# Two-layer transformer on one core: a fifth leaf of the MLP's Strassen products by inner products, and the first loads cut otherwise

## The chip, the core and the metric

The kernel runs as one program on one core of a Trainium2 chip. A core has a matrix engine (TensorE, PE in the profile, its weight loads PEld), VectorE (DVE), ScalarE (ACT), GpSimd (POOL) and SyncE (SP, which issues most DMA transfers). Each works through its own instruction list in order and waits on semaphores for the others. The metric is the device time of one execution in microseconds (us); given is the median of several executions.

## The reference

Two layers on 1024 tokens of width 1024 in float32: sliding-window attention with sinks, then a gated linear recurrence (HGRN2), each followed by an MLP with squared ReLU, and a last norm. What matters here is the MLP, which runs once in each layer:

```python
def rmsnorm(x, gain):
    y = xf * lax.rsqrt(jnp.mean(jnp.square(xf), axis=-1, keepdims=True) + NORM_EPS)
    return (y * gain.astype(jnp.float32)).astype(x.dtype)

def sqrelu_mlp(h, w_up, w_down):                     # 1024 -> 4096 -> 1024
    return jnp.square(jax.nn.relu(h @ w_up)) @ w_down

def reference(...):
    for layer in range(2):
        h = rmsnorm(x, mix_norm[layer])
        y = attention(h) if layer == 0 else hgrn2(h)
        x = x + y
        h = rmsnorm(x, mlp_norm[layer])
        x = x + sqrelu_mlp(h, mlp_w_up[layer], mlp_w_down[layer])
    return rmsnorm(x, final_norm)
```

## The kernel before

**Precision.** Every float32 operand is split into a high part in the fast float32r format and a low part, `lo = x - hi`, and a product takes three matmuls (`mm3`: hi*hi, hi*lo, lo*hi). Weights arrive by DMA in tiles `wr`; ScalarE casts the high part `wh`, VectorE subtracts to get the low part `wl` (`weight_split`, five buffers each). So each weight tile of 512 columns costs ScalarE one cast and VectorE one subtraction.

**Strassen in the MLP.** The up-projection goes over 16 pairs m of row blocks (m, m + 16) of 128 outputs each. One pair (`pair`) is a 2 x 2 Strassen-Winograd scheme with seven products (1 to 7), over output block, input half and token half. One product is four input tiles times three matmuls, so 12 matmuls with 512 token columns (`product`). The weight combinations s1 to s4 are made by VectorE in `m` buffers (six of them). The operands x[1] to x[7] on the token side are made once (`begin`, `finish`).

**Inner products.** From pair `INNER[layer]` on, some of the seven products are taken out of single pairs and done for two successive pairs at once by a second Strassen level. Such a *leaf* is called by the number of its product. For it the two weight blocks of both pairs (`up`, `low`) are combined by four half-width VectorE operations into four weight tiles ("12", "56", "73", "4"), and the four input tiles and two token halves into quarter operands (`inner_operands`). `inner_products` then does seven products of 2 x 3 matmuls of 256 columns, 42 instead of 2 x 12 of 512. After each of them VectorE adds the PSUM tile (128 x 256) to the sums of the pair. Before the change leaves 2, 3 and 4 are done so, from pair 2 on in layer 0 and from pair 4 on in layer 1. Leaves 2 and 4 keep their operands in SBUF; leaf 3 stores them to DRAM (`put_by`) and loads them into `t` buffers (18) for each use. In odd pairs leaf 2 and half of leaf 3 are done, in even ones leaf 4 and the rest of 3; the plain products 1, 5, 6, 7 stay in every pair.

**What sets the order.** The program is recorded as a list of operations with costs, and a planner (`Schedule`) places them engine by engine with list scheduling and several passes backward and forward. It knows the engines' costs, the hand-over times between them and the buffers, and takes a load as landed `LOAD` ns after its issue, a store as done `STORE` ns after it (3000 and 2000, behind an issue of 819 for 256 KB). Some operations may go to either of two engines: the squared ReLU of a sum (`square_relu`) is one operation on VectorE or two on ScalarE. The engines' lists are fixed when the program is built.

**Beginning and end.** The parameters (`par`: norm gains and lower bounds) come as 16 rows of 512 numbers by ScalarE's DMA queue, are turned into columns by four transposes on TensorE and copied to SBUF by ScalarE. Eleven dummy matmuls on zeros (`warm`) run ahead and between. Then the x tile of each input block is scaled by its gain on ScalarE (high part) and VectorE (low part), and the QKV products start; the first weight tile's high part is cast by VectorE. At the end (`final`) the last half block of 256 tokens is scaled in four tiles of 512 numbers per partition: one by GpSimd, which reads a copy of the scale factors that ScalarE makes from a second `spread` on TensorE, three by VectorE, one of them in two pieces; each piece has its own store.

In the profile all operations of the planner have line L433, so groups are told apart by tiles: `p` and `q` are the two sets of four PSUM banks, `wr`, `wh`, `wl`, `m`, `t`, `a` the buffers named above, `d` DRAM, `c` constants, `sm` small statistics.

Of the kernel before, what the change touches and what calls it, by code (L numbers as in the profile page):

```python
# [14 lines left out]
ALU = mybir.AluOpType  # L15
# [11 lines left out]
N_PAR = 8 * KT  # L27
# [109 lines left out]
LOAD, STORE = 3000.0, 2000.0  # L137
# [9 lines left out]
WARM = 11  # L147
ROWS = 16
EVACUATE = 100
HK = KT // 2  # L150
INNER = 2, 4
# [227 lines left out]
class Net:  # L379
# [129 lines left out]
    def weight_split(self, z, first=0, engines=("ACT",)):  # L509
        hi, lo = (self.tile(tag, BUFS[tag], (P, TH), F32R) for tag in ("wh", "wl"))  # L510
        c, n = slice(first, TH), TH - first
        self.copy(hi[:, c], z[:, c], n, engines, False)
        self.tt("any", lo[:, c], z[:, c], hi[:, c].bitcast(F32), ALU.subtract, n)
        return hi, lo
# [78 lines left out]
    def scaled(self, which, hf):  # L593

        h = []
        for kt in range(KT):
            x, gain = self.x[kt][hf], self.gain(which, kt)
            hi, lo = self.a(F32R), self.a(F32R)
            self.act(hi, x, AF.Copy, scale=gain)
# [9 lines left out]
    def square_relu(self, m, hf, c, psum):  # L609
# [6 lines left out]
        else:  # L616
# [7 lines left out]
            self.s.add({"ACT": (on_act, 2 * (94 + TH * 0.834) + 150), "DVE": (on_dve, 70 + TH * 1.04)}, [c], [c])  # L624
# [23 lines left out]
    def finish(self, which, upper_first=False, keep=False):  # L648

        x, t, q01, q11 = self.b, [], [], []  # L650
        self.u3 = []
# [6 lines left out]
        def lower():  # L658
            for j in range(HK):
# [3 lines left out]
                x[5].append(self.split(t[j]))  # L663

# [43 lines left out]
    def strassen_weights(self, first, second, done=(), inner=()):  # L708
# [15 lines left out]
        own = {2: a[0, 1], 3: s4}  # L724
# [12 lines left out]
        self.fourth = s4  # L737
# [4 lines left out]
    def inner_operands(self, own, kept, homes):  # L742
# [13 lines left out]
        new = lambda dt: self.t(dt, tag=next(homes))  # L756

        def split(name, z):
            y = self.split(z, new if homes else self.t)
            x[name] = [tuple(v[:, c] for v in y) for c in (L, R)] if homes else self.put_by(y)  # L760
# [28 lines left out]
    def inner_products(self, leaf, w, x, sums, steps):  # L789
# [6 lines left out]
        for step in steps:  # L796
            for name in step:
# [12 lines left out]
                self.tt("DVE", z, z, ps, ALU.add, 2 * P)  # L810
# [18 lines left out]
    def pair(self, m, x, leaves):  # L829
# [10 lines left out]
        if leaves and odd:  # L840
            inner.append((3, (self.fourth, 3), four if last else four[:2], (6, 9, 10, 11)))
            if last:
                inner.append((4, (up[m - 1 + half][:, TH:], up[m + half][:, TH:]), four, (9, 11, 13, 15)))
# [3 lines left out]
        w = self.strassen_weights(up[m], up[m + half], ((1, 2) if m < FIRSTS[self.layer] else ()) + ((2, 3, 4) if leaves else ()), inner)  # L847
# [37 lines left out]
        self.product(side, w[5], x[5], True)  # L885
        p5 = read(side)
# [3 lines left out]
        if leaves:  # L890
            self.tt("DVE", u2, u2, p5, ALU.add)
            self.sums[3].append((m, u2))
            if odd:
                z3 = self.rest = leaf(3, ((1, 2), (6, 5), (7, 3), (4,)))
# [19 lines left out]
        self.tt("any", p5, p5, u3, ALU.add)  # L914
        self.square_relu(m + half, 1, p5, False)
# [23 lines left out]
    def mlp(self, cut):  # L939

        x = self.mlp_second()
        for m in range(MT // 2):
            if m == INNER[self.layer]:
# [3 lines left out]
                                 4: self.inner_operands(self.b[4], self.u4, homes)}  # L947
                self.sums, self.rows = {2: [], 3: [], 4: []}, {}
# [46 lines left out]
    def down(self, cut):  # L995
# [99 lines left out]
        for c in (0, TH // 2):  # L1095
            tokens = slice(c, c + TH // 2)
# [78 lines left out]
    def first_loads(self):  # L1175
# [4 lines left out]
        rows = self.t()  # L1180
        self.op("ACT", self.nc.scalar.dma_start, [rows], [self.io["par"]], 100, rows[:ROWS], self.io["par"], tail=2900.0)
        ps = self.psum()
        n = N_PAR // ROWS
        for k in range(n):
            self.op("PE", self.nc.tensor.transpose, [ps], [rows, self.ident], 109, ps[:, k * ROWS : k * ROWS + ROWS],
                    rows[:ROWS, k * P : k * P + P], self.ident[:ROWS, :ROWS], form="whole")
        self.copy(self.par, ps[:, :N_PAR], N_PAR)
        for kt in range(KT):
            self.x[kt][0] = self.a()
            self.dma(self.x[kt][0], self.io["x"][0, kt], 4 * P * TH)  # L1190
# [6 lines left out]
    def qkv(self, hf, h, r, ahead=()):  # L1197

        blocks = range(hf * BPH, hf * BPH + BPH)
        for cg in range(3):  # L1200
            ps = {n: self.psum() for n in blocks}
            for kt in range(KT):
# [4 lines left out]
                w = self.weight_split(raw, engines=("ACT",) if kt or cg or hf else ("DVE",))  # L1207
# [679 lines left out]
```

## Time and profile before

| | us |
|---|---|
| median of 3 runs | 2060.28 (2060.0 to 2060.71) |
| the profiled execution, whole | 2058.19 |
| its span, first to last instruction | 2056.3 |
| TensorE clock granted (mean) | 0.999 |

| stage | about, us of the span |
|---|---|
| attention | 0 to 310 |
| MLP of layer 0, up-projection | 310 to 620 |
| its down-projection | 620 to 950 |
| HGRN | 950 to 1465 |
| MLP of layer 1, up-projection | 1465 to 1735 |
| its down-projection and the last norm | 1735 to 2056 |

The profile has several views. The page's head gives the busy time of each engine. *The chain of waits* goes back from the last instruction to what released it, and lists pieces as start, length, engine and tile, xcount. *Windows* give the busy time of each engine in a stretch. *Groups* collect equal instructions: busy time, mean ns of one, idle time of the engine before them and what ended it. *The timeline* lists instructions in order of time, equal ones merged. Matmuls overlap in the pipeline, so one's listed length is longer than its share of time; the pace is the length of a piece over its count.

### The profile page before, as it was taken

The page shows a single profiled execution, that of the slowest core. Times are in us where ns is not written, and L with a number is a line of the kernel's source. Part 1 is how long each engine was busy: PE and PEld are TensorE (multiplying, and loading weights), DVE is VectorE, ACT ScalarE, POOL GpSimd, SP SyncE. Part 2 cuts the span into 40 slices and gives each one's busy share as a digit, 9 for nine tenths or more (in the row PEclk, how much of TensorE's full clock was granted, in tenths as well). Part 3 has the DMA queues.
Part 4 walks back from the last instruction along what each step waited for, and adds up shares of the span by engine and source line. Part 5 has one row for each costly group of instructions (what it writes and reads, how often), then busy time and mean ns, then how long its engine had stood idle before and what let it go on. Part 6 is the DMA issues. An engine that isn't in the chain of part 4 may idle for free.

```text
span 2056.3 us, 35559 instructions
## 1 busy us (share of the span) xinstructions
PE 2046.4 (100%) x12150; PEld 1735.8 (84%) x12150; DVE 1845.8 (90%) x3699; ACT 1222.7 (59%) x2500; POOL 59.2 (3%) x121
## 2 busy tenths in 40 slices
PE   9999999999999999999999999999999999999998
PEld 8878888888898888888888888888888898888888
DVE  8899989999899979889988889998999899997985
ACT  7577977555565444666555555566765556444573
POOL 4030000000000000000000000000000000000000
PEclk9999999999999999999999999999999999999999
DMA  6212478877679978542333333688777677996812
GB/s 226 78 52 73 134 250 279 260 240 247 221 239 304 335 233 265 190 134 73 118 105 108 114 113 131 226 290 277 227 261 254 218 239 254 309 323 226 264 54 83
DMA packets 228486, 412.42 MB, mean 201 GB/s; under 512 B 25536, under 2 KB 30656, under 8 KB 228304
## 3 DMA queue, kind: packets, MB, share of 16 engines
q1 hardware_dynamic: 228272, 410.11, 60.0%
q8 instruction: 96, 1.57, 0.3%
q14 instruction: 86, 0.70, 0.1%
q10 hardware_dynamic: 32, 0.03, 0.0%
HBM read 319.34 MB, written 90.70 MB: 199 GB/s over the span
## 4 chain that ended last, share of the span: by engine, by line
PE 95%; DVE 2%; issue 1%; DMA 0%; ACT 0%; POOL 0%; POOLq 0%; DVEq 0%; ACTq 0%
PE p L433 49%; PE q L433 46%; DVE t L433 1%; DVE a L433 0%; DVE m L433 0%; DVE wl L433 0%; DMA d<-t 0%; DVE sm L433 0%; POOL a L433 0%; ACT m L433 0%; POOLq L1861 0%; ACT t L433 0%; DVEq L433 0%; POOLq L433 0%; ACTq L433 0%
## 5 line engine op out<-in xcount | busy, mean ns | idle before, releaser
L433 PE MATMUL p<-a,wh 128*128 128x512 f32 (+1 forms) x2680 | 751.9, 364 | 0.0
L433 PE MATMUL q<-a,wh 128*128 128x512 f32 x2180 | 673.8, 390 | 0.1
L433 PEld LDWEIGHTS p<-a,wh 128*128 128x128 f32 x2680 | 479.2, 189 | 78.5 <-DVE a L433 0.6
L433 PE MATMUL p<-a,wl 128*128 128x512 f32 (+1 forms) x1340 | 484.7, 362 | 0.0
L433 PEld LDWEIGHTS q<-a,wh 128*128 128x128 f32 x2180 | 402.7, 188 | 79.5 <-ACT t L433 0.5
L433 PE MATMUL q<-a,wl 128*128 128x512 f32 x1088 | 423.0, 389 | 0.0
L433 ACT CAST wh<-m 128x512 fp32r<-128x512 f32 (+1 forms) x336 | 205.3, 612 | 252.4 <-PE q L433 155.9
L433 ACT CAST wh<-wr 128x512 fp32r<-128x512 f32 (+1 forms) x323 | 194.6, 604 | 189.2 <-PE p L433 123.0
L433 PEld LDWEIGHTS p<-a,wl 128*128 128x128 f32 x1340 | 252.7, 189 | 37.2 <-DVE wl L433 0.4
L433 DVE TENSOR_TENSOR wl<-m,wh 128x512 fp32r<-128x512 f32 (+1 forms) x336 | 225.4, 676 | 55.4 <-ACT wh L433 51.1
L433 PEld LDWEIGHTS q<-a,wl 128*128 128x128 f32 x1088 | 204.3, 188 | 43.3 <-DVE wl L433 0.3
L433 DVE TENSOR_TENSOR wl<-wr,wh 128x512 fp32r<-128x512 f32 (+1 forms) x324 | 214.4, 665 | 21.3 <-ACT wh L433 19.0
L433 DVE TENSOR_TENSOR t<-t,t 128x512 f32<-128x512 f32 (+3 forms) x360 | 211.1, 607 | 15.1 <-ACT t L433 8.5
L433 DVE TENSOR_TENSOR a<-t,a 128x512 fp32r<-128x512 f32 (+1 forms) x317 | 209.1, 677 | 12.5 <-PE q L433 8.3
L433 ACT CAST a<-t 128x512 fp32r<-128x512 f32 (+1 forms) x237 | 141.6, 611 | 33.1 <-DVE t L433 10.6
L433 ACT ACTIVATE t<-t 128x512 f32<-128x512 f32 x196 | 123.6, 632 | 61.6 <-DVE t L433 58.1
L433 PE MATMUL p<-wh,a 128*128 128x512 f32 x384 | 124.8, 395 | 0.0
L433 DVE TENSOR_TENSOR m<-wr,wr 128x512 f32<-128x512 f32 (+1 forms) x186 | 120.3, 648 | 4.4 <-DMA wr<-in_down 3.1
L433 ACT COPY t<-q 128x512 f32<-128x512 f32 (+1 forms) x199 | 109.9, 558 | 23.2 <-PE q L433 11.5
L433 DVE TENSOR_TENSOR t<-t,p 128x256 f32<-128x256 f32 x273 | 111.3, 416 | 5.9 <-PE p L433 3.2
L433 ACT CAST a<-a 128x512 fp32r<-128x512 f32 x136 | 83.1, 620 | 49.5 <-DVE a L433 40.5
L433 DVE TENSOR_TENSOR a<-a,a 128x512 fp32r<-128x512 f32 (+2 forms) x151 | 101.0, 680 | 11.2 <-PE p L433 5.0
(135 smaller groups left out, 2428.2 us busy)
## 6 DMA issues: line engine op xcount, KB each, us to landing
t<-d SPq DMA_DIRECT2D x526, 256.0 KB, 4.3
d<-t SPq DMA_DIRECT2D x270, 256.0 KB, 3.0
wr<-in_down SPq DMA_DIRECT2D x224, 256.0 KB, 4.1
wr<-in_up SPq DMA_DIRECT2D x175, 256.0 KB, 3.9
a<-d SPq DMA_DIRECT2D x94, 256.0 KB, 4.6
wr<-in_win SPq DMA_DIRECT2D x68, 256.0 KB, 2.9
wr<-in_wqkv SPq DMA_DIRECT2D x48, 256.0 KB, 3.0
d<-a SPq DMA_DIRECT2D x48, 256.0 KB, 3.6
```

The lines of the kernel that those rows point to most:

```text
L433: fn(*[place(a) for a in args], **{k: place(v) for k, v in kw.items()})
```

## The change

1. **Fifth leaf.** Product 5 too is taken out of single pairs and done for two pairs by inner products, in the odd pair. Its operands are stored and loaded for each use, like leaf 3's (three of them; the others stay in SBUF), for which `finish` stores four more tiles (`u5`). The weight combination s1 of the even pair is held for the odd one (`self.fifth`). Four of its seven results are copied from PSUM by ScalarE (`fresh`), three are added by VectorE. The sums of both pairs are joined in the odd one (`upper_right`).
2. **Entry.** Layer 0 begins with leaves at pair 4 instead of 2; layer 1 as before at 4.
3. **Squares.** The squared ReLU of a sum goes to ScalarE alone.
4. **Planner.** `LOAD, STORE` from 3000, 2000 to 4200, 3200.
5. **Beginning.** The norm gains come as columns by one DMA (128 rows of 48 numbers), the lower bounds by a DMA of their own, later; transposes and copy go away. The first x tile is loaded and scaled in two halves, and the first weight tile's high part is cast half by VectorE, half by ScalarE. Nine dummies instead of eleven.
6. **End.** GpSimd's tile, the second `spread` and its copy go away for the last 256 tokens; VectorE does all four tiles, the first in two pieces.

```diff
-N_PAR = 8 * KT
+N_PAR = 6 * KT
-LOAD, STORE = 3000.0, 2000.0
+LOAD, STORE = 4200.0,3200.0
-WARM = 11
+WARM = 9
-INNER = 2, 4
+INNER = 4, 4
...
     def weight_split(self, z, first=0, engines=("ACT",), parts=False):
+        if parts:
+            for i, part in enumerate(PAIR):
+                self.copy(hi[:, part].only(i), z[:, part], TH // 2, engines[i : i + 1], False)
...
-            self.s.add({"ACT": (on_act, 2 * (94 + TH * 0.834) + 150), "DVE": (on_dve, 70 + TH * 1.04)}, [c], [c])
+            self.s.add({"ACT": (on_act, 2 * (94 + TH * 0.834) + 150)}, [c], [c])
...
     def inner_products(self, leaf, w, x, sums, steps, fresh=()):
-                self.tt("DVE", z, z, ps, ALU.add, 2 * P)
+                if name in fresh:
+                    self.copy(z, ps, 2 * P)
+                else:
+                    self.tt("DVE", z, z, ps, ALU.add, 2 * P)
...
         if leaves and odd:
-            inner.append((3, (self.fourth, 3), four if last else four[:2], (6, 9, 10, 11)))
+            inner.append((5, (self.fifth, 5), four, (5, 6, 7, 8)))
+            inner.append((3, (self.fourth, 3), four if last else four[:2], (9, 12, 13, 14)))
...
+        def upper_right(p5, n, u):
+            self.tt("any", p5, p5, u, ALU.add)
+            self.square_relu(n, 1, p5, False)
...
-        self.product(side, w[5], x[5], True)
-        p5 = read(side)
+        if not leaves:
+            self.product(side, w[5], x[5], True)
+            p5 = read(side)
+        elif odd:
+            early, p5 = (self.t() for _ in range(2))
+            run(self.inner_products(5, w, self.quarters[5], [early, p5], ((1, 2), (6, 5), (7, 3), (4,)), (1, 6, 5, 4)))
+            u = self.sums[3][-1][1]
+            self.tt("DVE", u, u, early, ALU.add)
+            upper_right(early, *self.sums[5][-1])
...
-        rows = self.t()
-        self.op("ACT", self.nc.scalar.dma_start, [rows], [self.io["par"]], 100, rows[:ROWS], self.io["par"], tail=2900.0)
-        ps = self.psum()
-        n = N_PAR // ROWS
-        for k in range(n):
-            self.op("PE", self.nc.tensor.transpose, [ps], [rows, self.ident], 109, ps[:, k * ROWS : k * ROWS + ROWS],
-                    rows[:ROWS, k * P : k * P + P], self.ident[:ROWS, :ROWS], form="whole")
-        self.copy(self.par, ps[:, :N_PAR], N_PAR)
+        self.op("ACT", self.nc.scalar.dma_start, [self.par], [self.io["par"]], 100, self.par, self.io["par"], tail=3000.0)
...
-        r, rs = self.spread(y, n), self.t()[:, :n]
-        self.copy(rs, self.spread(y, n) if ends else r, n)
+        r = rs = self.spread(y, n)
+        if not ends:
+            rs = self.t()[:, :n]
+            self.copy(rs, r, n)
...
-            e, share = ("DVE", r) if k else ("Pool", rs)
-            step = 1 if ends and k == per else per
+            e, share = ("DVE", r) if k or ends else ("Pool", rs)
+            step = 1 if ends and k == 0 else per
```

How the instructions move is shown at three places.

TensorE's list at the beginning of the program: dummies (from the zero tile `t`), the transposes of the parameter rows (to 128x16), then the first QKV products, four PSUM banks `p` each with matmuls on `wh` and `wl`. Before:

```order
L433 MATMUL p_178<-t_171 128x128 x6
L433 MATMUL p_208<-c_67,t_169 128x16 x4
L433 MATMUL p_178<-t_171 128x128 x5
L433 MATMUL p_243<-wh_214,a_225 128x512
L433 MATMUL p_243<-wl_222,a_225 128x512
L433 MATMUL p_243<-wh_214,a_236 128x512
L433 MATMUL p_253<-wh_214,a_225 128x512
L433 MATMUL p_253<-wl_222,a_225 128x512
```

After:

```order
L433 MATMUL p_177<-t_170 128x128 x9
L433 MATMUL p_225<-wh_215,a_220 128x512
L433 MATMUL p_225<-wl_218,a_220 128x512
L433 MATMUL p_234<-wh_215,a_220 128x512
L433 MATMUL p_234<-wl_218,a_220 128x512
L433 MATMUL p_239<-wh_215,a_220 128x512
L433 MATMUL p_239<-wl_218,a_220 128x512
L433 MATMUL p_225<-wh_215,a_230 128x512
L433 MATMUL p_234<-wh_215,a_230 128x512
L433 MATMUL p_239<-wh_215,a_230 128x512
```

The transposes and two dummies are gone. The first three banks take their matmuls with x's high part (`a_220`) first; those with its low part (`a_230`) follow.

TensorE's list in an odd pair of layer 1, a settled group: the first tile of leaf 2 (`wh`, `wl` of "12") times quarter operands `a`, into two banks. Before:

```order
L433 MATMUL p_20931<-a_17527,wh_20842 128x256
L433 MATMUL p_20931<-a_17548,wh_20842 128x256
L433 MATMUL p_20931<-a_17527,wl_20854 128x256
L433 MATMUL p_20931<-a_17541,wh_20842 128x256
L433 MATMUL p_20931<-a_17557,wh_20842 128x256
L433 MATMUL p_20931<-a_17541,wl_20854 128x256
L433 MATMUL p_20945<-a_17559,wh_20842 128x256
L433 MATMUL p_20945<-a_17566,wh_20842 128x256
L433 MATMUL p_20945<-a_17559,wl_20854 128x256
L433 MATMUL p_20945<-a_17572,wh_20842 128x256
L433 MATMUL p_20945<-a_17583,wh_20842 128x256
L433 MATMUL p_20945<-a_17572,wl_20854 128x256
```

After:

```order
L433 MATMUL p_20388<-a_17746,wh_20367 128x256
L433 MATMUL p_20388<-a_17776,wh_20367 128x256
L433 MATMUL p_20393<-a_17786,wh_20367 128x256
L433 MATMUL p_20393<-a_17802,wh_20367 128x256
L433 MATMUL p_20388<-a_17746,wl_20381 128x256
L433 MATMUL p_20388<-a_17761,wh_20367 128x256
L433 MATMUL p_20388<-a_17783,wh_20367 128x256
L433 MATMUL p_20388<-a_17761,wl_20381 128x256
L433 MATMUL p_20393<-a_17786,wl_20381 128x256
L433 MATMUL p_20393<-a_17794,wh_20367 128x256
L433 MATMUL p_20393<-a_17809,wh_20367 128x256
L433 MATMUL p_20393<-a_17794,wl_20381 128x256
```

Before, each bank's matmuls on the high and the low part of the weight alternate from the start. Now the first four rows are matmuls on the high part in both banks, and the first on the low part (`wl_20381`) comes behind them.

VectorE's list where layer 1's quarter operands are made (`t` with `t` at 256 columns, `a` the parts kept in SBUF) beside the weight tiles of the pairs that run (`wl`, `m`). Before:

```order
L433 TENSOR_TENSOR a_17548<-t_18109,a_17527 128x256
L433 TENSOR_TENSOR a_17557<-t_18109,a_17541 128x256
L433 TENSOR_TENSOR t_18109<-t_17914,t_18109 128x256
L433 TENSOR_TENSOR wl_18282<-wr_18063,wh_18273 128x512
L433 TENSOR_TENSOR t_18109<-t_17986,t_18109 128x256
L433 TENSOR_TENSOR m_18292<-wr_18075,wr_18222 128x512
L433 TENSOR_TENSOR a_18301<-t_18109,a_18294 128x512
L433 TENSOR_TENSOR t_18109<-t_17914,t_18109 128x256
L433 TENSOR_TENSOR t_18313<-t_18267 128x256
L433 TENSOR_TENSOR t_18313<-t_18138 128x256
L433 TENSOR_TENSOR m_18325<-wr_18222,wr_18279 128x512
L433 TENSOR_TENSOR wl_18332<-wr_18075,wh_18323 128x512
```

After:

```order
L433 TENSOR_TENSOR t_18484<-t_18365 128x256
L433 TENSOR_TENSOR wl_18489<-m_18459,wh_18479 128x512
L433 TENSOR_TENSOR a_17776<-t_18350,a_17746 128x256
L433 TENSOR_TENSOR a_17783<-t_18350,a_17761 128x256
L433 TENSOR_TENSOR t_18350<-t_18132,t_18350 128x256
L433 TENSOR_TENSOR t_18350<-t_18122,t_18350 128x256
L433 TENSOR_TENSOR t_18484<-t_18448 128x256
L433 SCALAR_TENSOR_TENSOR t_18450<-q_18211,t_18450 128x512
L433 TENSOR_TENSOR a_18530<-t_18350,a_18520 128x512
L433 TENSOR_TENSOR a_17563<-t_18484,a_17536 128x256
L433 TENSOR_TENSOR t_18350<-t_18132,t_18350 128x256
L433 TENSOR_TENSOR a_17572<-t_18484,a_17551 128x256
```

Before, operand work (`t_18109`, then `t_18313`) stands between weight work. Now two leaves' operands (`t_18350`, `t_18484`, the latter the new leaf's) stand in one row, with one weight operation among the twelve instead of four.

More of the change, by code (lines that the diff above doesn't have):

```diff
@@ L1094, in down @@
         yield 0, slice(0, TH)
-        for c in (0, TH // 2):
-            tokens = slice(c, c + TH // 2)
+        for tokens in PAIR:
             for m in range(HK):
```

69 lines of the change are left out of this document (44 added, 25 removed).

## Prediction

> **What bounds the kernel now.** I read the head of the page first, then the chain of waits, then the windows of the MLP's up-projection, then single rows at both ends.
>
> ```profile
> span 2056.3 us, 35559 instructions
> PE 2046.4 (100%) x12150; PEld 1735.8 (84%) x12150; DVE 1845.8 (90%) x3699; ACT 1222.7 (59%) x2500; POOL 59.2 (3%) x121
> PE 95%; DVE 2%; issue 1%; DMA 0%; ACT 0%; POOL 0%; POOLq 0%; DVEq 0%; ACTq 0%
> ```
>
> TensorE has work for the whole span, and 95% of the chain that ended last runs through it. A busy TensorE is not yet one at its pace, so the pace is read from the chain's pieces, which give a start, a length and a count:
>
> ```profile
> 786.98 43.52 PE p L433 x192
> 1570.81 2.87 PE p L433 x24
> 1573.68 2.75 PE q L433 x12
> 1576.42 2.15 PE p L433 x18
> ```
>
> The first piece is plain Strassen products of 512 tokens: 43.52/192 = 0.2267 us each. The others lie among the inner products of layer 1: 24 matmuls of 256 columns in 2.87 and 18 in 2.15, so 0.1195 each, and twelve of 512 columns in 2.75, 0.03 above 12 x 0.2267, once per change of width. These pieces follow each other without a hole, so TensorE sets the end and a removed matmul shortens the span. VectorE is the next engine. It has to deliver the low part of every weight tile:
>
> ```profile
> 1443.00:1480.00 37.00, 37.00 (x172) 30.55 (x171) 36.09 (x60) 27.73 (x51) 0.00 (x0) 1.00 0.69 224
> 1480.00:1517.00 37.00, 37.00 (x165) 30.63 (x164) 34.60 (x72) 26.70 (x52) 0.00 (x0) 1.00 0.81 274
> 1517.00:1554.00 37.00, 36.95 (x214) 32.39 (x213) 34.81 (x81) 21.56 (x39) 0.00 (x0) 1.00 0.78 251
> 1554.00:1591.00 37.00, 37.00 (x223) 33.08 (x222) 33.17 (x70) 20.10 (x36) 0.00 (x0) 1.00 0.70 233
> ```
>
> The columns after the length are the busy times of PE, PEld, DVE, ACT and POOL, then clock, DMA share and GB/s. In a settled stretch (the last row, about one group of two pairs) VectorE is busy 33.17 of 37; on entering layer 1's inner products (the first three) it has 0.9 to 2.4 us left in 37. So two things decide: how much matmul time goes, and whether VectorE still keeps ahead.
>
> **The change part by part. Matmuls.** A product of 512 tokens is 4 x 3 = 12 matmuls of 512 columns. By inner products two such products become 7 x 6 = 42 of 256. Layer 1 has six groups of two pairs and gains one leaf in each: 144 of 512 go, 252 of 256 come. Layer 0 had seven groups with three leaves (21) and now has six with four (24): 72 go, 126 come. Together 216 go, 378 come; the order has these counts. 378 x 0.1195 = 45.2 us come; 216 x 0.2267 = 49.0 go, or 49.5 at 2.75/12. That is -3.8 to -4.3. The changes of width from 512 to 256 fall from 133 to 126 in the order, worth 7 x 0.03 = 0.2, so I take **-4.0**.
>
> **The first 6 us.**
>
> ```profile
> 0.73 0.41 ACTq L433 DMA_DIRECT2D t<-in_par  x1
> 1.05 2.93 PE L433 MATMUL p<-t 128*128 128x128 f32 x12 [1.05 <-DVE t L433]
> 3.91 0.60 PE L433 MATMUL p<-c,t 16*128 16x16 f32 x4
> 4.00 0.61 DVE L433 CAST wh<-wr 128x512 fp32r<-128x512 f32 x1 [2.06 <-DMA wr<-in_wqkv]
> 4.44 2.01 PE L433 MATMUL p<-t 128*128 128x128 f32 x10
> 5.67 0.78 PE L433 MATMUL p<-t 128*128 128x128 f32 x5
> 4.79 0.72 ACT L433 ACTIVATE a<-a,c 128x512 fp32r<-128x512 f32 x1
> 6.20 0.48 PE L433 MATMUL p<-wh,a 128*128 128x512 f32 x1
> 6.79 0.72 ACT L433 ACTIVATE a<-a,c 128x512 fp32r<-128x512 f32 x1 [0.24 <-DMA a<-in_x]
> t<-in_par ACTq DMA_DIRECT2D x1, 32.0 KB, 2.9
> c<-in_pos SPq DMA_DIRECT2D x1, 4.0 KB, 4.7
> L433 ACT CAST wh<-wr 128x256 fp32r<-128x256 f32 x6 | 2.4, 407 | 1.5 <-PE p L433 1.5
> 2038.06 0.50 ACT L433 ACTIVATE a<-a,c 128x256 f32<-128x256 f32 x1
> ```
>
> Eleven dummies show as 22 passes, 12 before the four parameter transposes and 10 behind them; the first real matmul starts at 6.20, right behind the last dummy, though its operand was ready at 4.79 + 0.72 = 5.5. Twelve passes in 2.93 are 0.22 each; five in 0.78 from 5.67 on are almost twice as fast, so the array is slow until 5.67. Now there are nine dummies, 18 passes, and no transposes: 1.05 + 18 x 0.22 = 5.05. The operand: the first weight tile is there at 4.00, ScalarE splits its half in 0.41 and then makes the first half of x in 0.50, so 4.0 + 0.4 + 0.5 + about 0.1 = 5.0. The first real matmul starts at 5.05; until 5.67 it runs at half pace and loses 0.3. 6.20 - 5.05 - 0.3 = **-0.8**. The second x tile is issued one slot later (0.47 by the queue's rhythm), which can cost up to 0.4, and -1.1 is the gain with no slow stretch: bounds -1.1 and 0.
>
> The Trainium skill (TensorE: Matmul & The Clock Gate, Part 1) says that the warm-up is some 3.4 us of time and not a number of matmuls. The trace has 5.67 - 1.05 = 4.6 us, with transposes in between; by the page's figure the array would be fast before the last dummy and the term nearer -1.1, an estimate. The trace's own figure stays in the sum.
>
> **The end.**
>
> ```profile
> 2050.14 1.94 DVE L433 TENSOR_TENSOR a<-a,q 128x256 f32<-128x256 f32 x4 [0.87 <-PE q L433]
> 2051.03 1.27 POOL L433 TENSOR_TENSOR a<-a,t 128x512 f32<-128x512 f32 x1 [11.81 <-ACT t L433]
> 2038.59 14.67 SPq L433 DMA_DIRECT2D out<-a  x9
> ```
>
> GpSimd's tile, done at 2052.30, goes to VectorE, which is done with its own four at 2052.08 and takes 0.6 more: 2052.7. The last store was issued by 2053.26 and took 0.45 to issue, so from 2052.81; it now starts at about 2052.73: **-0.1**, bounds -0.2 and +0.3.
>
> **VectorE.**
>
> ```profile
> 1512.39 0.34 DVE a L433
> 1514.34 0.60 DVE wl L433
> L433 DVE SCALAR_TENSOR_TENSOR t<-t 128x512 f32<-128x512 f32 x13 | 8.9, 683 | 0.0
> L433 ACT CAST wh<-m 128x512 fp32r<-128x512 f32 x39 | 24.1, 619 | 33.9 <-PE q L433 21.3 <-issue 5.6 <-PE p L433 3.6
> 1528.49 0.68 DVE L433 TENSOR_TENSOR wl<-m,wh 128x512 fp32r<-128x512 f32 x1
> 1533.84 0.28 PE L433 MATMUL p<-t,wl 128*128 128x256 f32 x1
> ```
>
> Back to back a VectorE operation costs 0.60 at 512 columns and 0.34 at 256 (the chain's pieces). Per group there come three and a half low parts (2.1), four row sums (1.3) and three additions from PSUM (1.0); there go two low parts of the plain fifth products (1.2) and 13/3 squares, which are now ScalarE's alone (2.6). +0.7: 33.9 busy in a group that shrinks from 37.0 to 36.6 (72 x 0.2267 + 168 x 0.1195 + 6 x 0.03). ScalarE takes two activations for each square, four copies and the casts, some 7 us, to 27 of 36.6: hidden. ScalarE's own row says that its casts wait mostly for TensorE to give a buffer back (21.3 of 33.9), so VectorE in a settled group runs ahead as far as the five buffers let it. No wait there.
>
> The entry of layer 1's inner products is tighter. Priced row by row from the order, from the start of HGRN's output product to the first inner product, VectorE's work goes from 131.9 to 130.8 us and TensorE's from 152.7 to 147.5: the lead shrinks by 4.1, and at its lowest point in the pair behind it by 5.7. The smallest lead there is now 1533.84 - (1528.49 + 0.68) = 4.7 us, the last two rows. 4.7 - 5.7 leaves a wait of 1.0. VectorE's idle share there (2.2 to 2.4 in 37) can absorb some: I take **+0.7**, bounds 0 and 5.2 (the operands of the new leaf alone: ten of 0.34 and three of 0.60, if nothing absorbs them). Layer 0 enters two pairs later than before, behind pairs in which VectorE has half its time free: nothing there.
>
> **The transfers.** Three more stored operands of two tiles each are loaded per group: 1.6 MB on top of 233 GB/s x 37 us = 8.6 MB. The DMA share goes from 0.70 to about 0.84, which the second row above has (0.81) with TensorE unbroken. SP's later landings only reorder the issues: the plan gave a load 0.8 + 3.0 us.
>
> ```profile
> t<-d SPq DMA_DIRECT2D x526, 256.0 KB, 4.3
> ```
>
> It takes 4.3, so the plan was optimistic by 0.5 and TensorE did not wait for it; I cost it at nothing, with -2 (a wait or two less in attention and HGRN) and +2 as ends.
>
> **Sum.** 2056.3 - 4.0 - 0.8 - 0.1 + 0.7 = 2052.1 us of span. The profiled execution took 2058.19, 1.9 more than its span, and the median of the three runs is 2060.28; -4.2 on the median gives **2056.1**.
>
> **The rivals.** (B) *VectorE is late at layer 1's entry by 1.5 to 5 us.* For it: the three windows with 34.6 to 36.1 of 37, and the order, in which TensorE now takes the high-part matmuls of two banks before the first low part (second place shown with the change); against it: work before the entry can slip. With 3 us in place of 0.7: 2058.4. (C) *The parameters land late.* They come as 128 rows of 192 bytes. The only narrow load is c<-in_pos, 4.7 us against 2.9, though behind fourteen others. At 0.73 + 4.7 = 5.4 the half product ends at 5.9 and the first matmul starts at about 6.1: the first 6 us give 0.1, so 2056.8. The Trainium skill (DMA: Bandwidth & Descriptors, Specifications) puts the least transfer for full rate at 512 B; 24 KB are too little to tell by rate, and no run here shows it yet. (D) *The later landings remove waits elsewhere.* In HGRN the chain leaves TensorE for microseconds at a time:
>
> ```profile
> 1356.24 3.04 DVE t L433 x9
> 1362.25 0.65 PE L433 MATMUL q<-c,t 128*128 128x128 f32 x4 [0.73 <-DVE t L433]
> ```
>
> At the end of that stretch TensorE waits 0.73. A second wait of that length and some shorter ones gone, 1.8 us, would give 2054.3. Against it: this wait is on VectorE, and not on a landing. (E) *VectorE becomes the bound of every group.* If the 3.8 us that it idles in 37 cannot be filled, a group lasts 33.9 + 3.8 = 37.7 instead of 37.0: twelve times +0.7, and the thirteenth, all plain now (168 x 0.2267 = 38.1), +1.1, gives +9.5 where -4.0 stood: 2060.28 - 0.9 + 9.5 = 2068.9. It decides as soon as more than 36.6 - 33.9 = 2.7 of that idle time is not to be filled. Against it: the buffer waits of ScalarE above.
>
> **How the numbers follow.** About 0.2%, 4.1 us, is what a measurement here tells from no change; below 2056.2 counts as faster. Forecast 0.47 (2054.9 to 2057.0; 0.29 of it below the line, since the dearer 512 price and a lead that holds both lie on that side, 0.18 above), B 0.20, C 0.07, D 0.18, E 0.08. Faster 0.29 + 0.18 = 0.47; within 0.18 + 0.20 + 0.07 = 0.45; slower 0.08. The range: 2053.2 (D with a full startup gain) to 2060.6 (B at its far end); E lies outside.
>
> **What would show it.** 216 fewer matmuls of 512 and 378 more of 256 at 0.227 and 0.1195; the first p<-wh,a near 5.05; the last store issued near 2052.7 less what is gained. VectorE busy about 33.9 in a settled group with TensorE unbroken. Holes in front of matmuls on a low part between layer 1's first inner products and two pairs later are B; holes in every group are E, and would make the prediction wrong.

## The result and the profile after

| | before | after |
|---|---|---|
| median, us | 2060.20 (8 runs, 2059.55 to 2062.34) | 2054.83 (8 runs, 2054.41 to 2055.12) |
| ratio | | 0.9973, 95% interval 0.9964 to 0.9982 |
| the profiled execution, whole | 2058.19 | 2054.78 |
| its span | 2056.3 | 2053.0 |

The change is faster by 5.4 us in the median. 2056.1 was predicted, with a range of 2053.2 to 2060.6; 2054.83 lies in the range, just below the 2054.9 to 2057.0 that the prediction gives to the forecast itself. The profiled executions differ by 3.4 us only; where the other 2 us come from is the main question of the experiments.

The head of the page of after, and its chain of waits by engine:

```profile
span 2053.0 us, 36250 instructions
PE 2042.3 (99%) x12300; PEld 1740.3 (85%) x12300; DVE 1853.4 (90%) x3751; ACT 1289.1 (63%) x2647; POOL 56.1 (3%) x120
PE 93%; DVE 6%; issue 1%; ACT 0%; DVEq 0%; ACTq 0%
```

TensorE still sets the end. The pace comes from two pieces of the chain (start, length, engine and tile, count):

```profile
1704.72 5.75 PE p L433 x48
1906.28 43.52 PE p L433 x192
```

43.52/192 = 0.2267 for 512 columns, as before; 5.75/48 = 0.1198 for 256. In the traces there are 6772 product matmuls of 512 columns (6988 before) and 2464 of 256 (2086 before): the 216 and 378 of the prediction. They are worth 378 x 0.1198 - 216 x 0.2267 = -3.7 us.

The windows of a settled stretch of layer 1's inner products, four groups long: start and end, length, then the busy times of PE, PEld, DVE, ACT and POOL, clock, DMA share and GB/s. Before:

```profile
1554.00:1702.00 148.00, 148.00 (x889) 132.33 (x888) 133.10 (x277) 79.86 (x142) 0.00 (x0) 1.00 0.71 233
```

After:

```profile
1549.00:1695.40 146.40, 146.28 (x961) 134.18 (x961) 137.89 (x310) 103.37 (x194) 0.00 (x0) 1.00 0.86 283
```

Per group of 36.6 us VectorE is now busy 137.89/4 = 34.5 us and ScalarE 25.8; TensorE has 0.12 us of holes in four groups. The waits of TensorE in after (in total, times, longest):

```profile
PE q L433 <- DVE sm L433: 1.4, 1, 1.4
PE p L433 <- DVE t L433: 1.0, 1, 1.0
PE q L433 <- ACT m L433: 0.5, 1, 0.5
PE p L433 <- DVE a L433: 0.3, 1, 0.3
PE q L433 <- ACT t L433: 0.2, 1, 0.2
PE q L433 <- issue: 0.2, 1, 0.2
```

The first two are the last norm and the start. So the trace of after has few waits left that could be removed, none above 0.5 us outside its beginning and end. Its beginning:

```profile
1.05 4.21 PE L433 MATMUL p<-t 128*128 128x128 f32 x18 [1.05 <-DVE t L433]
3.82 0.40 ACT L433 CAST wh<-wr 128x256 fp32r<-128x256 f32 x1 [1.37 <-DMA wr<-in_wqkv]
4.29 0.91 ACT L433 ACTIVATE a<-a,c 128x256 fp32r<-128x256 f32 x2
4.91 0.77 PE L433 MATMUL p<-wh,a 128*128 128x512 f32 x1
6.36 0.63 PE L433 MATMUL p<-wl,a 128*128 128x512 f32 x1
6.79 0.53 PE L433 MATMUL p<-wh,a 128*128 128x512 f32 x1
7.16 0.39 PE L433 MATMUL p<-wl,a 128*128 128x512 f32 x1
```

The first product matmul starts at 4.91 instead of 6.20, as the prediction has it (5.05). But the array works at half pace until 7.16 (from 6.36 to 6.79 it takes 0.43 us from one matmul to the next, later 0.23), where the profile of before had it fast from 5.84 on, in the last dummies (the first instruction that takes the short time to the next one). The table follows a few places of the program through both traces:

| start of, us | before | after | difference |
|---|---|---|---|
| first product matmul | 6.20 | 4.91 | -1.3 |
| 13th | 9.06 | 8.77 | -0.3 |
| 193rd | 51.73 | 51.92 | +0.2 |
| last attention values | 264.90 | 264.58 | -0.3 |
| last inner product of layer 0 | 610.77 | 609.46 | -1.3 |
| last inner product of layer 1 | 1733.67 | 1730.07 | -3.6 |
| last matmul | 2050.27 | 2046.22 | -4.1 |
| end of the span | 2056.31 | 2052.97 | -3.3 |

Between these two executions the beginning brings nothing, the leaf brings what its matmuls are worth, and the end gives 0.7 back (some 0.45 of it only because the last four matmuls of the old end are gone, so that the last matmul is an earlier one).

### The profile page after: what moved, and what is told of

Same layout as the page of the kernel before. It is cut to its first block, busy times and chain, and to the rows that moved or that the text cites. A ratio compares the mean times of both kernels' runs of the same rounds, so it can differ in the third digit from the quotient of the medians.

```text
span 2053.0 us, 36250 instructions
## 1 busy us (share of the span) xinstructions
PE 2042.3 (99%) x12300; PEld 1740.3 (85%) x12300; DVE 1853.4 (90%) x3751; ACT 1289.1 (63%) x2647; POOL 56.1 (3%) x120
## 4 chain that ended last, share of the span: by engine, by line
PE 93%; DVE 6%; issue 1%; ACT 0%; DVEq 0%; ACTq 0%
PE p L433 50%; PE q L433 43%; DVE t L433 3%; DVE a L433 1%; DVE wl L433 1%; DVE m L433 1%; DVE sm L433 0%; ACT t L433 0%; ACT m L433 0%; ACT L433 0%; ACT wh L433 0%; ACT a L433 0%; DVEq L1892 0%; ACT sm L433 0%; DVEq L433 0%
## 5 line engine op out<-in xcount | busy, mean ns | idle before, releaser
L433 PE MATMUL p<-a,wh 128*128 128x512 f32 (+1 forms) x2832 | 781.1, 361 | 0.2
L433 PE MATMUL q<-a,wh 128*128 128x512 f32 x2020 | 625.9, 390 | 0.0
L433 PEld LDWEIGHTS p<-a,wh 128*128 128x128 f32 x2832 | 500.8, 189 | 79.0 <-ACT wh L433 1.0
L433 PEld LDWEIGHTS q<-a,wh 128*128 128x128 f32 x2020 | 375.0, 188 | 74.2 <-DVE a L433 0.2
L433 PE MATMUL q<-a,wl 128*128 128x512 f32 x1008 | 391.8, 389 | 0.0
L433 DVE TENSOR_TENSOR wl<-m,wh 128x512 fp32r<-128x512 f32 x354 | 234.6, 667 | 38.9 <-ACT wh L433 32.9
L433 DVE TENSOR_TENSOR wl<-wr,wh 128x512 fp32r<-128x512 f32 (+1 forms) x324 | 214.0, 665 | 18.6 <-ACT wh L433 17.2
L433 DVE TENSOR_TENSOR a<-t,a 128x512 fp32r<-128x512 f32 (+2 forms) x321 | 210.2, 674 | 18.0 <-ACT a L433 6.8
L433 ACT ACTIVATE t<-t 128x512 f32<-128x512 f32 x288 | 179.6, 631 | 69.1 <-DVE t L433 64.1
L433 ACT COPY t<-q 128x512 f32<-128x512 f32 (+2 forms) x174 | 95.2, 556 | 24.3 <-PE q L433 19.0
L433 PEld LDWEIGHTS q<-t,t 128*64 128x64 f32 (+1 forms) x2160 | 95.8, 144 | 13.5 <-issue 7.3
```

Source lines behind the costliest of these rows:

```text
L433: fn(*[place(a) for a in args], **{k: place(v) for k, v in kw.items()})
```

## Experiments: the parts alone

Four kernels beside one another: the new beginning alone, the new numbers in the planner alone, the fifth leaf alone (with its later entry in layer 0 and the squares on ScalarE), and the change once more. The numbers alone are one line:

```diff
-LOAD, STORE = 3000.0, 2000.0
+LOAD, STORE = 4200.0,3200.0
```

The leaf alone is the change with this line, the beginning and the end put back; the beginning alone is item 5 of the change put into the kernel before.

Expected of the leaf alone:

> The fifth leaf, layer 0's entry at pair 4 and the squares on ScalarE alone, on the kernel before; old beginning, old landings, old end. Sum (the forecast's own terms): -4.0 for matmuls and +0.5 to +0.7 for waits on VectorE, so -3.3 to -3.5 us against before. Landings or Beginning (the rest of the measured -5.4 comes from one of these): the same -3.4 here, since neither is in this kernel. If it shows -5 or more, the leaf alone explains the result and the term was too small.

Of the beginning alone:

> The beginning alone (parameters as columns, first x tile in halves, nine dummies) on the kernel before. Sum: -0.3 to -0.8 us; the first real matmul near 4.9 instead of 6.2. Beginning: -2 us, because the timed executions of before lose more at the start than its profiled one did. Landings: -0.3 as in the trace.

Of the planner's numbers alone:

> LOAD and STORE of 4200 and 3200 alone on the kernel before: no instruction added or removed, only another order. Sum: 0, within 0.5 us. Landings: -1.5 to -2 us, and runs that scatter less than those of before. Beginning: 0.

Of the change again:

> The changed kernel once more on the same chip, as the measure for the parts: all theories -4.5 to -5.5 us against before. Its profile is a second look at the first 8 us: if the moment at which the array becomes fast belongs to the kernel it is again near 7.2; if it is a matter of the execution it lies elsewhere.

| kernel | median, us (range, runs) | ratio to before, 95% |
|---|---|---|
| before | 2060.29 (2057.78 to 2064.37, 28) | |
| leaf alone | 2059.51 (2055.92 to 2062.69, 11) | 0.9984 to 1.0002 |
| beginning alone | 2059.44 (2057.78 to 2061.32, 11) | 0.9986 to 1.0004 |
| planner's numbers alone | 2059.59 (2058.30 to 2060.66, 11) | 0.9986 to 1.0004 |
| the change again | 2054.69 (2054.37 to 2055.37, 6) | 0.9959 to 0.9982 |

No part alone is told from before, and together they would make -2.3 where the whole makes -5.6. The leaf alone misses its expectation most: its fastest execution is 1.9 us under the fastest of before, its median 0.8 where 3.3 to 3.5 was expected (the interval just reaches 3.3). The beginning alone, -0.85, is just beyond the end of what "Sum" said (-0.8); the numbers alone, -0.7, lie between their two theories; the whole, -5.6, is just beyond the -5.5 expected. The ranges tell more than the medians: kernels with the old numbers scatter by 3.5 to 7 us, the numbers alone by 2.4, the change by 1.

## Experiments: the parts taken out

The second set takes one part out of the change at a time, so that with the first all eight combinations of leaf, beginning and numbers are there. The change with the old numbers is the line above read backward; the change with the old beginning is item 5 undone; beginning and numbers without the leaf are the two parts put into the kernel before. The fourth kernel is before itself, for the profile of another execution.

> The change with one line put back: LOAD, STORE = 3000, 2000 (fifth leaf, new beginning and new end stay). Theory Sum (each part is worth what it brought alone; the landings alone brought 0.7 us): 2055.4 us, scatter as narrow as the change's (1 us). Theory Leaf needs landings (the planner takes a load as landed after 0.8 + 3.0 us, the loads of stored operands take 4.3 to 4.5, and with the fifth leaf's loads on top VectorE and ScalarE start late by a different amount in each execution): 2057 to 2059 us, a scatter of 4 us or more, waits of VectorE and ScalarE for transfers of over 15 us in the trace where the change has some 14, and holes in TensorE's list of 0.3 to 1.6 us inside the MLPs; its fastest execution near the change's median.

> The change with the old beginning (parameters as 16 rows with four transposes, whole first x tile, eleven dummies); leaf, landings and new end stay. Theory Sum: the beginning alone brought 0.85 us, so 2055.5 us. Theory Beginning (the profiled execution of before had an early start by luck, its array at full pace at 5.7 us; two other executions of the same beginning reached it only at 8.7 and 9.0, and their 13th product matmul came at 10.6 us and not at 9.1): 13th product matmul at 10.6 us, median 2056.2 to 2056.8, scatter up to 1.5 us. Theory Landings alone decide: 2054.7 to 2055.0.

> The kernel before with the new beginning and with LOAD, STORE = 4200, 3200; no fifth leaf, old end. Theory Sum of the parts alone: 0.85 + 0.7 = 1.55 below before, 2058.7 us. Theory Leaf is worth its matmuls and no more once nothing waits: the change's median plus 3.8 to 4.0 for the 216 and 378 matmuls, minus up to 0.7 for the entry and the end: 2057.9 to 2058.6 us, scatter of 1 us. If the beginning and the landings by themselves bring the larger part of the 5.6 us: below 2057.5.

> The kernel before as it is, for the profile of another execution. If the profiled execution shown of before was a lucky one at its beginning: first product matmul at 6.6 to 6.9 us instead of 6.20, the array at full pace at 8.5 to 9.0 us instead of 5.67, the 193rd product matmul near 53.3 us instead of 51.73, span 2057 to 2060. If not: 6.2, 5.7, 51.7, and a span that differs only through waits further on.

All eight, with the time that VectorE and ScalarE wait for transfers in the profiled execution (summed over the rows of the view of waits), and the start of the 193rd product matmul:

| beginning | numbers | leaf | median, us (range, runs) | waits for transfers, us | 193rd matmul, us |
|---|---|---|---|---|---|
| old | old | no | 2060.29 (2057.78 to 2064.37, 28) | 28.1; again 39.0 | 51.73; again 53.90 |
| new | old | no | 2059.44 (2057.78 to 2061.32, 11) | 39.7 | 52.16 |
| old | new | no | 2059.59 (2058.30 to 2060.66, 11) | 10.8 | 53.59 |
| old | old | yes | 2059.51 (2055.92 to 2062.69, 11) | 47.2 | 53.27 |
| new | new | no | 2058.30 (2057.76 to 2059.07, 11) | 16.4 | 51.79 |
| new | old | yes | 2058.88 (2056.33 to 2062.37, 11) | 48.3 | 51.91 |
| old | new | yes | 2054.85 (2054.75 to 2056.70, 6) | 9.7 | 52.29 |
| new | new | yes | 2054.83 (2054.41 to 2055.12, 8) | 15.9 | 51.92 |

In the second set before had 2061.27 (22 runs); the ratios were 0.9979 to 0.9996 for the change with the old numbers, 0.9958 to 0.9982 with the old beginning, 0.9978 to 0.9996 without the leaf.

**The leaf needs the numbers.** With the new beginning and the old numbers the leaf brings 2059.44 - 2058.88 = 0.6 us, with the new numbers 2058.30 - 2054.83 = 3.5. In the other direction the numbers bring 1.1 us without the leaf and 4.1 with it. "Sum" falls, "Leaf needs landings" holds: median, scatter and waits came out as it said (only the fastest execution with the old numbers, 2056.33, stays 1.6 us above the change's median, and the largest hole of TensorE lies in HGRN and not in an MLP). And 2058.30 without the leaf is what the matmuls alone let expect.

The sizes are less sure than the direction, since these differences go across sets. Before itself had 2060.29 in the first and 2061.27 in the second. Taken each against the before of its own set (and the change from the first set, 2054.69), the leaf brings 1.5 us with the old numbers and 2.6 with the new, the numbers 2.1 without it and 3.2 with it. The traces leave out the beginning and the end if one goes from the 193rd product matmul to the first matmul of the last scale factors. Over that stretch the leaf takes 3.8 us away with the new numbers and the new beginning, 3.5 with the new numbers and the old beginning; with the old numbers it adds 1.1 and 1.0. Each is one execution against one, and the two executions of before differ by 2.1 us there.

The waits of the change with the old numbers show how; first some of the largest of VectorE and ScalarE for transfers (total, times, longest):

```profile
DVE m L433 <- DMA wr<-in_up: 3.5, 3, 2.0
DVE m L433 <- DMA a<-in_wg: 2.0, 1, 2.0
ACT a L433 <- DMA t<-d: 12.9, 15, 1.8
ACT wh L433 <- DMA wr<-in_up: 7.3, 7, 3.1
```

The place, in HGRN, from the timeline (start, length, engine and operation; in brackets the idle time before it and what ended it):

```profile
1328.90 0.69 DVE L433 TENSOR_TENSOR m<-wr,a 128x512 f32<-128x512 f32 x1 [1.96 <-DMA a<-in_wg]
1330.36 0.49 PE L433 MATMUL q<-t,m 128*128 128x128 f32 x2 [1.76 <-DVE m L433]
```

In after there is no row for wr<-in_up or a<-in_wg at either engine, and ScalarE's largest for stored tiles are these:

```profile
ACT wh L433 <- DMA t<-d: 2.1, 1, 2.1
ACT a L433 <- DMA t<-d: 2.0, 3, 1.1
ACT t L433 <- DMA a<-d: 1.3, 1, 1.3
```

A tile lands late, VectorE (or ScalarE) starts late, and TensorE behind it. TensorE's own rows name VectorE or ScalarE here and not the transfer, so the view of TensorE's waits alone doesn't show the cause. A second such stop of 0.88 us stands in this trace at 1559.60, in layer 1's inner products, behind a wr<-in_up that VectorE waited for until 1555.69. TensorE's waits add up to 8.0 us in this trace and to 3.6 in that of after, and the spans differ by 5.5. The new profile of before has the same chain of three engines:

```profile
395.23 0.42 DVE L433 TENSOR_TENSOR m<-m,wr 128x256 f32<-128x256 f32 x1 [2.83 <-DMA wr<-in_up]
397.62 1.30 ACT L433 ACTIVATE t<-t 128x512 f32<-128x512 f32 x2 [2.88 <-DVE t L433]
399.97 0.50 PE L433 MATMUL q<-a,wh 128*128 128x512 f32 x1 [1.59 <-ACT t L433]
```

The first profile of before has nothing at this place. The two executions have the same instructions, so they can be compared matmul by matmul: the second is 2.2 us behind at the 193rd product matmul, 1.75 more are lost at this place and 0.3 at a wait in HGRN, and the last matmul is 4.3 behind. So the beginning makes half of this difference and one late landing most of the rest. That the scatter of all the runs is made of the same two things is argued from this pair, not shown run by run.

The sum of the feeding engines' waits is not the time lost. The beginning alone has 39.7 us of them, and TensorE's own waits are 4.4 us there, against 4.0 and 6.1 in the two executions of before. With the leaf and the old numbers they are 6.6 and 8.0, in the four kernels with the new numbers 3.6 to 4.1.

**The old beginning has two outcomes.** Its kernels with the new numbers, which scatter little otherwise (the new beginning has 1.3 and 0.7 us there), fall into two groups: without the leaf four runs from 2058.30 to 2058.68 and seven from 2059.55 to 2060.66, with the leaf five runs from 2054.75 to 2055.19 and one at 2056.70. Five traces of this beginning have the array fast from 5.84 and 6.04 us on (193rd matmul at 51.73 and 52.29), or from 8.99, 8.99 and 10.56 (53.27 to 53.90). The new profile of before (span 2060.6, one run of 2062.46) has the late one that was expected, and later still, at 10.56:

```profile
4.04 0.58 PE L433 MATMUL p<-c,t 16*128 16x16 f32 x4
4.55 2.50 PE L433 MATMUL p<-t 128*128 128x128 f32 x10
6.70 0.77 PE L433 MATMUL p<-wh,a 128*128 128x512 f32 x1
8.98 0.63 PE L433 MATMUL p<-wh,a 128*128 128x512 f32 x1
```

In the two early ones the transposes follow the dummies at 3.91; in the three late ones at 4.04 to 4.18, and one of them names the reason, the profile of the new numbers alone:

```profile
4.18 0.58 PE L433 MATMUL p<-c,t 16*128 16x16 f32 x4 [0.20 <-DMA t<-in_par]
```

So parameters that are 0.13 to 0.27 us late go with an array that is slow for some 3 to 4.5 us more. Five traces show that the two go together, and not that one causes the other. The nine traces of the new beginning have the array fast between 4.38 and 7.17 (the change itself at 7.16 and, in its second profile, at 6.17, so the moment belongs to the execution and not to the kernel), and yet the 193rd matmul between 51.79 and 52.36. Where the array is early, here the kernel without the leaf, it stands still for the second x tile instead:

```profile
1.05 3.93 PE L433 MATMUL p<-t 128*128 128x128 f32 x18 [1.05 <-DVE t L433]
4.74 0.50 PE L433 MATMUL p<-wh,a 128*128 128x512 f32 x1
8.20 0.50 PE L433 MATMUL p<-wh,a 128*128 128x512 f32 x1 [0.46 <-ACT a L433]
```

The theory of the beginning was right about the two outcomes and wrong about how often: the change with the old beginning has a median of 2054.85 and not 2056.2 or more. By the median "Landings alone decide" came out; by their times five of the six runs had the early outcome and the one of 2056.70 the late one, but only one of the six was traced (an early one). So the new beginning is worth nothing against a good start and 1.4 to 2 us against a bad one.

## Experiments: which landing, later still, and the end

Three kernels change the planner's numbers in the change, the fourth puts the old end back (item 6 undone):

```diff
-LOAD, STORE = 4200.0,3200.0
+LOAD, STORE = 4200.0,2000.0
...
-LOAD, STORE = 4200.0,3200.0
+LOAD, STORE = 3000.0,3200.0
...
-LOAD, STORE = 4200.0,3200.0
+LOAD, STORE = 5000.0,4000.0
```

> The change with LOAD, STORE = 4200, 2000: only the planned end of a store is put back (after it a stored tile may be loaded again). Theory Loads decide (the waits that the old numbers left are of VectorE and ScalarE for tiles that come in, t<-d, wr<-in_up, a<-in_wg): 2054.7 to 2055.2 us, as the change. Theory Stores decide (stored operands are loaded again before their store is done): 2057 to 2059 us with 4 us of scatter, as with both numbers old (2058.88). Theory Both, half each: 2056 to 2057.

> The change with LOAD, STORE = 3000, 3200: only the planned landing of a load is put back. Theory Loads decide: 2057.5 to 2059 us, scatter of 4 us or more, over 30 us of waits of VectorE and ScalarE for transfers in the trace. Theory Stores decide: 2054.7 to 2055.2. Theory Both, half each: 2056 to 2057.

> The change with LOAD, STORE = 5000, 4000, later still. If the gain of the later landings is the removal of waits and these are gone (the change's trace has no wait of TensorE above 0.45 us outside its beginning and end): 2054.4 to 2055.2 us, no gain. If loads that land late still cost: below 2054.2. If buffers held longer bind (a load issued earlier holds its buffer longer): 2055.5 to 2058.

> The change with the old end (GpSimd takes one tile of four, four matmuls and a copy more). Theory of the prediction (the last store starts 0.1 us earlier with the new end): 2054.8 us, the old end 0.1 dearer. Theory Other way round (from the first matmul of the last scale factors to the end of the span it was 6.88 us in three traces with the old end and 7.16 in two of the new, with 2.04 less to the last addition or not; two other traces of the new end had 6.59 and 6.87): 2054.4 to 2054.6 us. Below 2054.3 it would beat the change by more than a measurement here tells.

| LOAD, STORE, end | median, us (range, runs) | ratio to before, 95% | waits for transfers, us |
|---|---|---|---|
| before in this set | 2060.46 (2057.91 to 2065.07, 22) | | |
| 4200, 2000, new | 2056.87 (2055.51 to 2057.36, 11) | 0.9974 to 0.9991 | 17.2 |
| 3000, 3200, new | 2057.69 (2054.68 to 2065.82, 11) | 0.9977 to 0.9999 | 37.5 |
| 5000, 4000, new | 2053.68 (2053.51 to 2054.55, 5) | 0.9952 to 0.9979 | 6.4 |
| 4200, 3200, old | 2054.86 (2054.35 to 2055.22, 6) | 0.9961 to 0.9984 | 14.8 |

**Both numbers count.** The old store costs 2.0 us, the old load 2.9, both together 4.1. For the store "Both" came out, for the load "Loads decide". The scatter comes with the load: 11 us against 2, or 4 without its two slowest runs (2063.98 and 2065.82), in which the granted clock was 0.996 and 0.997 instead of 0.999; what lowered it there was not recorded. With the old store the largest row of ScalarE's waits for transfers is for stores:

```profile
ACT t L433 <- DMA d<-t: 6.8, 8, 2.1
```

With the old load it is for loads of stored tiles:

```profile
ACT a L433 <- DMA t<-d: 12.6, 11, 3.6
```

These numbers move the whole order and not only the transfers, so a part of each 2 to 3 us may lie in other moves; that was not separated.

**Later still is faster.** 5000, 4000 gives 2053.68, 1.0 to 1.2 us below the change; only the slowest of its five runs is within the range of the change's fourteen, though the intervals against before overlap. The expectation by which no wait was left to remove missed by 0.7, and the one below 2054.2 came out. Its profiled execution is that slowest run, with one wait that the change hasn't, in front of HGRN:

```profile
PE p L433 <- ACT t L433: 1.0, 1, 1.0
```

Part of the gain can still be read from this trace: its 193rd matmul comes 0.4 us later than in after, its first inner product of layer 0 0.5 us earlier (400.37 against 400.88). Of after's small holes in attention (0.13 to 0.47 us, 0.9 in all, between 130 and 240 us) one of 0.21 is left. None of them can be followed back to a transfer in the trace of after, so this part seems to come from another order. Whether the other four runs lack the wait of 1.0 us no trace shows; without it this one would be at 2053.5, as they are. It is the fastest kernel of the study.

**The end is worth nothing.** 2054.86 against 2054.83 and 2054.69. The last matmuls, additions and stores of after:

```profile
2045.81 0.68 PE L433 MATMUL q<-c,sm 128*128 128x128 f32 x4 [1.36 <-DVE sm L433]
2046.53 2.54 DVE L433 TENSOR_TENSOR a<-a,q 128x256 f32<-128x256 f32 x5 [0.87 <-PE q L433]
2047.01 2.46 SPq L433 DMA_DIRECT2D out<-a  x5
```

And the matmuls of before:

```profile
2049.42 1.13 PE L433 MATMUL q<-c,sm 128*128 128x128 f32 x8 [1.36 <-DVE sm L433]
```

The last store is issued by 2049.47, 3.66 us behind the first of these matmuls; before it was 2053.26 - 2049.42 = 3.84. The 0.1 us of the prediction is there and a little more (0.18), and the landing and the closing instructions behind it take 0.45 longer in this pair of executions: 3.50 us from the last issue to the end of the span (2052.97 - 2049.47) instead of 3.05. Why, the profile doesn't show.

## Why the prediction was right, point by point

- **Matmuls, -4.0.** The counts are exact, the durations 0.2267 and 0.1198 in place of 0.1195: -3.7 and the changes of width.
- **VectorE, +0.7.** At layer 1's entry TensorE's excess over its pace (from the starts of its matmuls) is 0.18 us at 1526 and 0.29 at 1602, 0.5 in all. In the settled group VectorE is busy 34.5 of 36.6 (33.9 predicted), ScalarE 25.8 (27), and TensorE doesn't wait. Rival E is out, rival B too. Both terms together, -3.3, stand against 2054.83 - 2058.30 = -3.5 measured with the other parts in place (-2.6 if each is taken against the before of its set).
- **The first 6 us, -0.8.** The first product matmul came at 4.74 to 5.03 in all nine traces of the new beginning, so the timing of operands and dummies was right (2.93/12 is 0.24 and not 0.22, but the passes start 0.213 apart behind a first one of 0.375, which gives the same 5.05). The step "it runs at half pace until 5.67" took the moment at which the array becomes fast from one execution as if it belonged to the kernel. It moves between 4.38 and 10.56. The mean of the 193rd matmul is 52.96 us in five traces of the old beginning and 52.04 in nine of the new, -0.9; alone it brought 0.85 in the median (an interval that takes in zero), without the leaf and with the new numbers 1.3, in the whole 0. The size fits on the average, not in any one pair of executions, and that it does is luck. Rival C is out: the parameters landed in 3.3 us, from 0.73 on, and nothing waited for them.
- **The end, -0.1.** Not to be told from nothing.
- **Transfers and later landings, 0 (-2 to +2).** This is the step that failed. "the plan was optimistic by 0.5 and TensorE did not wait for it; I cost it at nothing": VectorE and ScalarE waited for transfers, 28 us in all in the trace of before, and stand in front of TensorE. That none of these waits can be followed on to a stop of TensorE in that trace was the luck of that execution; in the other one 1.6 us can. The numbers bring 0.7 us alone, 1.1 with the new beginning and 4.1 with the leaf (2.1 and 3.2 against the before of their sets), beyond the bound of -2. They also decide whether the -4.0 of the first term arrives: with the old numbers most of it doesn't (0.6, or 1.5). The term was priced as a part beside the others, and it is what the leaf stands on. In a settled group the DMA share went to 0.86 (0.84 predicted), from 0.71.
- **The base.** The sum was made against a span of 2056.3 and carried to a median 2.1 us above that execution, as if that distance stayed. It was, as far as the two executions of before show it, late landings and slow starts: the kernel with the new beginning and numbers alone has a median of 2058.30, the time of that execution (2058.19). The change takes them away, and all eight runs of after have spans of 2052.6 to 2053.3. In spans the sum was 0.9 too good (2052.1 against 2053.0), since this execution of before had the good beginning; in the medians it was 1.3 too poor. So the result lies within the range through a right leaf and, by luck, two errors that partly cancel: the beginning, which gave nothing in the profiled pair, and the base. Rival D, with its 2054.3, was nearest in size, and right in that later landings remove waits. Its example was not such a wait: in the trace of before VectorE works without a stop ahead of the 0.73 us at 1362.25, so the objection to it was right there. That wait is gone with the numbers alone all the same, by another order; the late landings that cost time were elsewhere. The range's lower end, 2053.2, takes the beginning off twice (2054.3 already holds 0.8 of the 1.1; it should be 2054.0), and the result is above both.

The 5.4 us of the medians can be put together in one order from the tables: beginning and numbers without the leaf 2060.29 - 2058.30 = 2.0, the leaf behind them 3.5, the end 0. Against the before of the second set the first part is 3.0 (2061.27 - 2058.30), which leaves 2.4 for the leaf, so this split is good to about 1 us.

## What to carry to other kernels

When an engine that feeds the bounding one waits for transfers, look at its waits too, even if the bounding engine shows none: not all of that time is lost, but it shows where an added load can turn a late landing into a stop, and a change that adds loads and one that issues loads earlier are to be priced together. A planner's landing times want the measured ones or more (loads of stored tiles took 4.3 to 4.5 us in the median where 3.8 was planned; 5.0 and 5.8 were both better). One profiled execution whose time lies 2 us under the median is a sample of the good case, and a term read from it needs a second one.

## What the hardware showed beyond that

The array's full pace came at a time that differs between executions of identical instructions (7.16 and 6.17 in the change, 5.84 and 10.56 in before): with unbroken dummies from 1.05 us on, 3.3 to 6.1 us later in nine traces; with the short stop for the parameters 4.8 to 9.5 us later in five. The Trainium skill (TensorE: Matmul & The Clock Gate, Part 1) says that the clock is released after a busy window of some 3.4 us, and that these windows run freely and don't begin with the kernel. The nine traces agree with that: about one window at the least and not quite two at the most; the prediction weighed the 3.4 us against the trace's 4.6 and not that the windows run freely. The 7.9 to 9.5 us of the three late starts are more than two such windows; whether a stop that is 0.13 to 0.27 us longer spoils a whole window no run here shows.
